# Wide weight splits, fp32r sums over partitions, late norm sums and heads of four in a three-block network

## The chip, the cores and the metric

The kernel runs on one core of a Trainium2 chip. A core has TensorE (matmuls, 128 x 128 stationary operand, results in PSUM), VectorE, ScalarE, GpSimd and SyncE, which run side by side and meet through semaphores; DMA queues bring data from HBM. The metric is the device time of one execution in microseconds (us), the median of several runs.

## The reference

One sequence of 512 positions, width 1024, goes through three blocks and everything is fp32. Cut to its skeleton:

```python
def first_block(x, mem, ...):           # one layer
    proj = _rmsnorm(x, g_in) @ w_in
    o_a = _nsa_mixer(...) * silu(gate_a)        # compressed, block-selected and windowed attention
    o_b = _ssd_mixer(...)                       # chunked state-space scan, conv of 4, RMS norm
    o_c = _memory_attention(...) * silu(gate_x) # cross attention to mem
    return _rmsnorm(x + concat([o_a, o_b, o_c]) @ w_out, g_final)

def second_block(x, ...):               # conv of 31 and gated recurrence (hgrn), mixed
    x = layer_norm(ALPHA * x + mix @ w_out, ...)
    return layer_norm(ALPHA * x + (gelu(conv3(u)) * gv) @ w_ffn_out, ...)

def third_block(x, ...):                # two layers
    for layer in range(2):
        x = x + 0.5 * rms_norm(swiglu(rms_norm(x, g[0]), ...), g[1])
        h = rms_norm(x, g[2])
        h = mlstm_mixer(h, ...) if layer == 0 else diff_attention(h, k_sh, v_sh, ...)
        x = x + rms_norm(h, g[3])
        x = x + 0.5 * rms_norm(swiglu(rms_norm(x, g[4]), ...), g[5])
        gate = sigmoid(rms_norm(x, g[6]) @ w_ple_gate[layer])
        x = x + rms_norm((p[layer] @ w_ple_proj[layer]) * gate, g[7])
        if layer == 0: k_sh, v_sh = shared_kv(x, ...)
    return x
```

## The kernel before

The state x lies transposed: eight tiles of 128 features by 512 positions. Every large product is made from split operands. An fp32 array a is kept as a `Pair` of float32r (fp32r) arrays, hi (a copy that rounds, on ScalarE) and lo = a - hi (on VectorE); `mm3` (lines 125 to 127) makes a product of three fp32r matmuls, hi x hi, hi x lo and lo x hi, that add up in one PSUM bank. `weight` (line 107, its copies on lines 112 and 113) loads up to 1024 columns of weights into one of three raw buffers and splits them in pieces of 512 columns into a ring of 12 hi and 12 lo tiles.

`linear` (line 160) makes output tiles m of 128 features: for each m it runs over the contraction tiles k, then calls the evacuation that takes the PSUM bank away. There are six banks for this and two more (`bank2`) for small things. Two kinds of groups are special. A *head* of 3 or 4 output tiles is run interleaved, k outside and m inside, first on positions 0 to 255 and then on 256 to 511, so that it can use x tiles in halves as they come. A *tail* of 2 or 3 tiles is run with the first half of the positions of all its tiles ahead of the second, so that the norm over the outputs can finish for the first half while the second is multiplied.

Norms divide by a root of a sum over features. `Norm.square` (line 345) squares a tile on ScalarE, `Sums.add` (line 315) adds the squares of the tiles on GpSimd, and a matmul with a matrix of ones in plain fp32 sums over the partitions and spreads the sum to all of them: `Sums.total` (line 328) for what has been added up, line 320 for the last tile where `late` is set. The profile shows such an fp32 matmul as two instructions. `rsqrt` (lines 269 to 273) makes the reciprocal root on ScalarE and corrects it with three VectorE instructions. `Layer` does the same for layer norms.

After each sublayer `post` (lines 461 and 462) updates x for the first half of the positions and all eight tiles, then for the second, and calls `then` for each piece. Mostly that is `Pre.feed`: it splits the piece, scaled by the next norm's gain (lines 142 and 143), and hands it to `Norm.square` for the next norm. The next product uses the split x without the norm's factor; the factor (`pre.row`) is multiplied in at the evacuation. Where the norm is *lazy*, `linear` finishes it half by half, each behind its half of the head's matmuls. `Pre.feed` runs behind eight such posts, once at full width in the first block and once at full width for the second layer of block three.

The queues are not written out by hand. Tile buffers are rings, and a scheduler at build time gives each engine its order of instructions: of those whose inputs and buffers are there by its own cost model, the one that comes first in the program. At run time each engine keeps that order, and an instruction that waits holds back those behind it on its engine.

## Time and profile before

| | us |
|---|---|
| median of three runs | 3583.32 (3582.47 to 3584.28) |
| the profiled execution | 3585.29 |
| its span, first to last instruction | 3583.5 |
| TensorE busy | 3483.7 (97%) |
| VectorE busy | 2055.7 (57%) |
| ScalarE busy | 1539.3 (43%) |
| GpSimd busy | 485.6 (14%) |
| mean granted TensorE clock | 0.989 of full speed |

An engine counts as busy while it has an instruction in work. TensorE's instructions overlap, so that its busy share says that it had work, not how fast it went. "PEld" is the loading of stationary operands, which runs beside the matmuls. Idle time is put down to the instruction whose result was waited for.

### The profile page before, as it was taken

How to read it: one execution, taken by the hardware profiler on the slowest of the kernel's cores; microseconds unless marked ns; L12 is line 12 of the kernel's file. 1: busy time of each engine (PE TensorE's matmuls, PEld its weight loads, DVE VectorE, ACT ScalarE, POOL GpSimd, SP SyncE). 2: the span in 40 equal slices, each digit the busy share in tenths (PEclk: the TensorE clock that was granted, in tenths of full speed). 3: DMA queues.
4: the chain of work that ended last, by engine and by line, in shares of the span. 5: the costliest groups of instructions: out<-in, count | busy, mean ns of one | idle time of the engine just before them, and what ended most of it. 6: DMA issues, size and time to landing. Idle time of an engine off the chain costs nothing. (4 is left out here: it accounts for less than half of the span.)

```text
span 3583.5 us, 48642 instructions
## 1 busy us (share of the span) xinstructions
PE 3483.7 (97%) x18454; PEld 2924.8 (82%) x18454; DVE 2055.7 (57%) x3879; ACT 1539.3 (43%) x2879; POOL 485.6 (14%) x509
## 2 busy tenths in 40 slices
PE   8999899999999999999999999998999999999997
PEld 7677798888788888888887888887888887888886
DVE  6677669895456354633384763439443448673337
ACT  5465544663434243433345443336433335443335
POOL 2000011230110001201110220114010111020112
PEclk9999999999999999999999999999999999999999
DMA  4411242112323333332321133222533323123331
GB/s 146 127 32 58 62 134 77 53 48 74 109 78 101 99 99 96 108 98 95 96 87 60 60 104 102 91 87 83 188 95 100 93 84 94 56 89 96 98 95 65
DMA packets 109714, 323.97 MB, mean 90 GB/s; under 512 B 12328, under 2 KB 28456, under 8 KB 109480
## 3 DMA queue, kind: packets, MB, share of 16 engines
q1 hardware_dynamic: 93648, 299.27, 26.5%
q10 hardware_dynamic: 15832, 21.60, 1.8%
q8 instruction: 145, 2.38, 0.3%
q14 instruction: 89, 0.73, 0.1%
HBM read 308.23 MB, written 12.58 MB: 90 GB/s over the span
## 5 line engine op out<-in xcount | busy, mean ns | idle before, releaser
L125 PE MATMUL ps<-x,hi 128*128 128x512 f32 (+1 forms) x3552 | 1292.3, 366 | 6.6 <-ACT x L142 5.2
L126 PE MATMUL ps<-x,hi 128*128 128x512 f32 (+1 forms) x3552 | 1279.7, 361 | 9.3 <-DVE x L143 8.6
L127 PE MATMUL ps<-x,lo 128*128 128x512 f32 (+1 forms) x3552 | 1275.0, 360 | 1.6 <-DVE lo L113 1.6
L112 ACT CAST hi<-raw 128x512 fp32r<-128x512 f32 (+1 forms) x1112 | 668.8, 612 | 1265.9 <-PE ps L126 1119.8
L113 DVE TENSOR_TENSOR lo<-raw,hi 128x512 fp32r<-128x512 f32 (+1 forms) x1112 | 784.8, 715 | 714.3 <-ACT hi L112 712.1
L126 PEld LDWEIGHTS ps<-x,hi 128*128 128x128 f32 x3552 | 674.8, 190 | 113.2 <-DVE x L143 16.3
L125 PEld LDWEIGHTS ps<-x,hi 128*128 128x128 f32 x3552 | 671.5, 190 | 107.6 <-ACT x L142 9.2
L127 PEld LDWEIGHTS ps<-x,lo 128*128 128x128 f32 x3552 | 673.6, 190 | 101.8 <-issue 2.5
L125 PE MATMUL ps<-h,hi 128*128 128x512 f32 (+1 forms) x990 | 367.1, 371 | 0.0
L127 PE MATMUL ps<-h,lo 128*128 128x512 f32 (+1 forms) x990 | 364.0, 368 | 0.0
L126 PE MATMUL ps<-h,hi 128*128 128x512 f32 (+1 forms) x990 | 361.2, 365 | 0.0
L485 POOL TENSOR_TENSOR gt<-gt,gt 128x512 f32<-128x512 f32 x88 | 137.7, 1566 | 1090.3 <-DVE gt L484 954.8
L127 PEld LDWEIGHTS ps<-h,lo 128*128 128x128 f32 x990 | 185.8, 188 | 34.3
L126 PEld LDWEIGHTS ps<-h,hi 128*128 128x128 f32 x990 | 185.9, 188 | 33.2
L125 PEld LDWEIGHTS ps<-h,hi 128*128 128x128 f32 x990 | 186.2, 188 | 30.6
L315 POOL TENSOR_TENSOR sqa<-sqa,sq 128x256 f32<-128x256 f32 (+1 forms) x171 | 166.1, 971 | 293.8 <-ACT sq L345 285.6
L140 DVE TENSOR_TENSOR h<-gt,h 128x512 fp32r<-128x512 f32 x110 | 76.7, 700 | 148.9 <-ACT h L139 146.9
L139 ACT CAST h<-gt 128x512 fp32r<-128x512 f32 x110 | 68.1, 620 | 182.6 <-POOL gt L485 174.4
L484 DVE TENSOR_TENSOR gt<-ps,rbc 128x512 f32<-128x512 f32 x88 | 60.7, 690 | 119.4 <-PE ps L127 119.4
L143 DVE SCALAR_TENSOR_TENSOR x<-x,c,x 128x256 fp32r<-128x256 f32 (+1 forms) x144 | 96.5, 676 | 22.4 <-ACT x L142 22.4
L479 DVE TENSOR_TENSOR gt<-ps,rbc 128x512 f32<-128x512 f32 x88 | 60.8, 690 | 79.9 <-PE ps L127 78.6
L142 ACT ACTIVATE x<-x,c 128x256 fp32r<-128x256 f32 (+1 forms) x144 | 75.4, 528 | 72.4 <-DVE x L462 57.3
(630 smaller groups left out, 3975.4 us busy)
## 6 DMA issues: line engine op xcount, KB each, us to landing
raw<-fi SPq DMA_DIRECT2D x220, 512.0 KB, 3.5
raw<-fo SPq DMA_DIRECT2D x80, 512.0 KB, 3.5
raw<-fo SPq DMA_DIRECT2D x80, 192.0 KB, 2.3
raw<-out SPq DMA_DIRECT2D x16, 512.0 KB, 3.6
raw<-qf SPq DMA_DIRECT2D x16, 512.0 KB, 3.6
raw<-mz SPq DMA_DIRECT2D x16, 512.0 KB, 3.5
raw<-pg SPq DMA_DIRECT2D x16, 512.0 KB, 3.5
raw<-mr SPq DMA_DIRECT2D x9, 512.0 KB, 3.6
```

What stands on the lines that cost most here:

```text
L112: nc.scalar.copy(hi[:, :b], raw[:, a:a + b])
L113: nc.vector.tensor_tensor(lo[:, :b], raw[:, a:a + b], hi[:, :b].bitcast(F32), ALU.subtract)
L125: mm(out, lhs.hi, rhs.hi, start=start, stop=False)
L126: mm(out, lhs.hi, rhs.lo, start=False, stop=False)
L127: mm(out, lhs.lo, rhs.hi, start=False, stop=stop)
L139: nc.scalar.copy(hi, x)
L140: nc.vector.tensor_tensor(lo, x, hi.bitcast(F32), ALU.subtract)
L142: nc.scalar.mul(hi, x, g)
L143: nc.vector.scalar_tensor_tensor(lo, x, g, hi.bitcast(F32), ALU.mult, ALU.subtract)
L315: nc.gpsimd.tensor_tensor(self.acc[:, sl], self.part[h][:, sl], s[:, sl], ALU.add)
L479: nc.vector.tensor_tensor(t, q, pre.row, ALU.mult)
L485: nc.gpsimd.tensor_tensor(u, u, hold[0], ALU.mult)
```

## The change

- `weight` splits a load of up to 1024 columns with one copy and one subtraction into one of 6 hi and 6 lo tiles of 1024 columns. `linear` cuts a contraction of 11 or 12 tiles into loads of 6 (before: of 8).
- The sum over partitions, `ones_sum`, splits its operand into an fp32r pair and takes two fp32r matmuls with an fp32r matrix of ones. The split tiles share the ring of the squares, which grows from 2 to 3 buffers. The layer norm's sum of centred squares stays as it is.
- The adds of `Sums.add` go to VectorE where they are half a tile wide or where the norm is marked `fast`; at full width the others stay on GpSimd.
- `Pre.feed` only splits. `Pre.finish` squares all eight x tiles at full width, adds them on VectorE and finishes the norm; `linear` calls it behind both halves of the head, ahead of the evacuations.
- The mLSTM's first product and the gate product have heads of 4 instead of 3; the gate's tail has 2 tiles instead of 3.

```diff
-        self.wsp = e(tc.tile_pool(name="wsp", bufs=12))
+        self.wsp = e(tc.tile_pool(name="wsp", bufs=6))
...
+        self.onesr = self.const.tile([P, P], F32R, name="onesr")
+        nc.scalar.copy(self.onesr, self.ones)
...
-        bufs = 4 if tag == "gt" else bufs
+        bufs = {"gt": 4, "sq": 3}.get(tag, bufs)
...
-        ps = []
-        for a in range(0, n, 512):
-            b = min(512, n - a)
-            hi = self.wsp.tile([P, 512], F32R, tag="hi", name=self.name("hi"))
-            lo = self.wsp.tile([P, 512], F32R, tag="lo", name=self.name("lo"))
-            nc.scalar.copy(hi[:, :b], raw[:, a:a + b])
-            nc.vector.tensor_tensor(lo[:, :b], raw[:, a:a + b], hi[:, :b].bitcast(F32), ALU.subtract)
-            ps.append(Pair(hi, lo))
-        return ps
+        hi = self.wsp.tile([P, 1024], F32R, tag="hi", name=self.name("hi"))
+        lo = self.wsp.tile([P, 1024], F32R, tag="lo", name=self.name("lo"))
+        nc.scalar.copy(hi[:, :n], raw[:, :n])
+        nc.vector.tensor_tensor(lo[:, :n], raw[:, :n], hi[:, :n].bitcast(F32), ALU.subtract)
+        return Pair(hi, lo)
...
+    def ones_sum(self, q, s, sl, start, stop):
+        nc = self.nc
+        p = Pair(*(self.tmp.tile([P, 512], F32R, tag="sq", name=self.name("os"), bufs=3)[:, sl] for _ in range(2)))
+        nc.scalar.copy(p.hi, s[:, sl])
+        nc.vector.tensor_tensor(p.lo, s[:, sl], p.hi.bitcast(F32), ALU.subtract)
+        nc.tensor.matmul(q[:, sl], self.onesr, p.hi, start=start, stop=False)
+        nc.tensor.matmul(q[:, sl], self.onesr, p.lo, start=False, stop=stop)
...
+        step = kt if kt <= 8 else 6
...
-                    if pre and pre.norm.lazy:
-                        pre.norm.finish(sl)
+                if pre:
+                    pre.finish()
                 for m in ms:
                     evac(m, qs[m], FULL)
...
-            self.acc = self.acc or c.t512("sqa", bufs=3)
-            nc.gpsimd.tensor_tensor(self.acc[:, sl], self.part[h][:, sl], s[:, sl], ALU.add)
+            self.acc = self.acc or c.t512("sqa", bufs=2)
+            eng = nc.gpsimd if sl == FULL and not self.fast else nc.vector
+            eng.tensor_tensor(self.acc[:, sl], self.part[h][:, sl], s[:, sl], ALU.add)
...
-            nc.tensor.matmul(self.q[h][:, sl], c.ones, s[:, sl], start=False, stop=True)
+            c.ones_sum(self.q[h], s, sl, False, True)
...
-        self.c.nc.tensor.matmul(q[:, sl], self.c.ones, self.part[hs[0]][:, sl], start=True, stop=stop)
+        self.c.ones_sum(q, self.part[hs[0]], sl, True, stop)
...
-        self.norm = Norm(c, len(x), late=False, lazy=lazy)
+        self.norm = Norm(c, len(x), late=False, lazy=True, fast=True)
 
     def feed(self, k, sl=FULL):
         self.xg[k] = self.c.split(self.x[k], self.g[:, k:k + 1], tag=f"x{k}", into=self.xg[k], sl=sl)
-        self.norm.square(self.x[k], sl)
+
+    def finish(self):
+        if self.norm.row is None:
+            for t in self.x:
+                self.norm.square(t)
+            self.norm.finish()
...
-        c.linear(w_rows, KD, pre.xg, ev, head=3, pre=pre)
+        c.linear(w_rows, KD, pre.xg, ev, head=4, pre=pre)
...
-        c.linear(w_gate, KD, pre.xg, ev, head=3, tail=3, pre=pre)
+        c.linear(w_gate, KD, pre.xg, ev, head=4, tail=2, pre=pre)
```

## Rows read from the trace of the kernel before

**Rows 1.** The page's first part: busy time (share of the span) and instructions.

```profile
PE 3483.7 (97%) x18454; PEld 2924.8 (82%) x18454; DVE 2055.7 (57%) x3879; ACT 1539.3 (43%) x2879; POOL 485.6 (14%) x509
```

**Rows 2.** Busy time of each engine (x instructions) in stretches around the heads.

```profile
core 0: us, PE busy (x) PEld busy (x) DVE busy (x) ACT busy (x) POOL busy (x), PEclk, DMA share, GB/s
1053.00:1077.00 24.00, 24.00 (x198) 23.87 (x197) 18.69 (x51) 9.98 (x26) 0.00 (x0) 1.00 0.14 44
1436.00:1465.00 29.00, 28.02 (x214) 26.84 (x212) 20.43 (x43) 18.48 (x46) 9.09 (x10) 1.00 0.20 66
1806.00:1831.00 25.00, 21.35 (x154) 19.21 (x153) 25.00 (x50) 13.96 (x36) 12.49 (x26) 1.00 0.00 1
2052.00:2076.00 24.00, 23.56 (x183) 22.17 (x182) 24.00 (x46) 12.60 (x33) 10.85 (x14) 1.00 0.00 1
2417.00:2444.00 27.00, 22.86 (x160) 20.11 (x159) 27.00 (x53) 14.44 (x37) 10.73 (x14) 1.00 0.13 40
2476.00:2510.00 34.00, 29.80 (x201) 27.89 (x202) 33.34 (x58) 22.00 (x50) 18.05 (x19) 0.90 0.12 40
2952.00:2982.00 30.00, 24.43 (x161) 21.48 (x160) 28.48 (x58) 15.65 (x38) 13.73 (x18) 0.95 0.14 41
```

**Rows 3.** Timeline of TensorE, 512 columns: start, duration, instruction.

```profile
400.21 0.39 PE L127 MATMUL ps<-x,lo 128*128 128x512 f32 x1
400.44 0.39 PE L125 MATMUL ps<-x,hi 128*128 128x512 f32 x1
```

**Rows 4.** Timelines of VectorE and GpSimd in a post and at the kernel's end.

```profile
1808.50 0.47 DVE L143 SCALAR_TENSOR_TENSOR x<-x,c,x 128x256 fp32r<-128x256 f32 x1
...
1810.50 1.00 DVE L143 SCALAR_TENSOR_TENSOR x<-x,c,x 128x256 fp32r<-128x256 f32 x1
...
1810.49 3.36 POOL L315 TENSOR_TENSOR sqa<-sqa,sq 128x256 f32<-128x256 f32 x4 [0.53 <-ACT sq L345]
...
3578.59 0.74 DVE L461 TENSOR_TENSOR gt<-e,rbc 128x256 f32<-128x256 f32 x2
3579.26 0.86 DVE L462 SCALAR_TENSOR_TENSOR x<-gt,c,x 128x256 f32<-128x256 f32 x2
```

**Rows 5.** TensorE's waits: us in total, times, longest.

```profile
PE pt L328 <- POOL sqa L315: 26.8, 25, 6.7
```

**Rows 6.** Groups at full width: xcount, busy us, mean ns, idle before.

```profile
L345 ACT ACTIVATE sq<-x 128x512 f32<-128x512 f32 x22 | 13.6, 626 | 6.0 <-POOL sqa L315 5.5 <-DVE x L953 0.4
...
L113 DVE TENSOR_TENSOR lo<-raw,hi 128x512 fp32r<-128x512 f32 x1032 | 740.5, 728 | 665.1 <-ACT hi L112 662.9 <-PE ps L127 0.7 <-PE pt L240 0.5
...
L270 ACT ACTIVATE rbc<-pt,cc 128x512 f32<-128x512 f32 x8 | 5.5, 687 | 3.7 <-PE pt L320 3.5 <-PE pt L328 0.2
```

**Rows 7.** Timeline of TensorE at a full-width and a half-width fp32 sum.

```profile
45.89 1.02 PE L328 MATMUL pt<-sqa,ones 128*128 128x512 f32 x2
46.34 0.68 PE L125 MATMUL ps<-x,hi 128*128 128x256 f32 x1
46.86 0.28 PE L126 MATMUL ps<-x,hi 128*128 128x256 f32 x1
...
2466.79 0.60 PE L320 MATMUL pt<-sq,ones 128*128 128x256 f32 x2
2467.04 0.47 PE L126 MATMUL ps<-x,hi 128*128 128x256 f32 x1
2467.34 0.28 PE L127 MATMUL ps<-x,lo 128*128 128x256 f32 x1
```

**Rows 8.** Groups of half-width fp32 sums by shape; two instructions make a sum.

```profile
L328 PE MATMUL pt<-sqa,ones 128*128 128x256 f32 x78 | 26.7, 425 | 20.1 <-POOL sqa L315 20.1
...
L320 PE MATMUL pt<-sq,ones 128*128 128x256 f32 x36 | 12.7, 437 | 0.0
...
L320 PE MATMUL pt<-x,ones 128*128 128x256 f32 x8 | 2.6, 412 | 0.0
```

**Rows 9.** Busy time and granted clock (PEclk) in a stretch, as rows 2.

```profile
2501.00:2505.00 4.00, 3.79 (x20) 3.79 (x21) 4.00 (x8) 2.02 (x5) 2.21 (x2) 0.58 0.40 135
```

More of the change, by code (lines that the diff above doesn't have):

```diff
@@ L160, in mm @@
             def mm(m, k, sl):
-                if (m, k // 8) not in ws:
-                    a = k // 8 * 8
-                    ws[m, k // 8] = self.weight(w[m][:, a * P:min(a + 8, kt) * P])
-                o = (k % 4) * P
-                self.mm3(qs[m][:, sl], ws[m, k // 8][k % 8 // 4][:, o:o + P], x[k][:, sl], k == 0, k == ks[-1])
+                c = k // step
+                if (m, c) not in ws:
+                    ws[m, c] = self.weight(w[m][:, c * step * P:min(c * step + step, kt) * P])
+                o = (k - c * step) * P
+                self.mm3(qs[m][:, sl], ws[m, c][:, o:o + P], x[k][:, sl], k == 0, k == ks[-1])
             first = head and ms[0] == 0
@@ L197, in linear_t @@
                     wt = self.weight(w[cb, k // 2])
-                rhs = wt[k % 2]
+                rhs = wt[:, k % 2 * 512:k % 2 * 512 + 512]
                 for t in range(nt):
@@ L294, with __init__ @@
 class Sums:
-    def __init__(self, c, n, late):
-        self.c, self.n, self.late = c, n, late and n > 1
+    def __init__(self, c, n, late, fast=False):
+        self.c, self.n, self.late, self.fast = c, n, late and n > 1, fast
         self.left = [n, n]
@@ L334, with __init__ @@
 class Norm:
-    def __init__(self, c, n, eps=EPS, late=True, lazy=False):
+    def __init__(self, c, n, eps=EPS, late=True, lazy=False, fast=False):
         self.c, self.n, self.eps, self.lazy = c, n, eps, lazy
-        self.sums = Sums(c, n, late and not lazy)
+        self.sums = Sums(c, n, late and not lazy, fast)
         self.row = None
@@ L411, in parts @@
         for k in range(kt):
-            c.mm3(q, t[4][k // 4][:, k % 4 * P:(k % 4 + 1) * P], x[k], k == 0, k == kt - 1)
+            c.mm3(q, t[4][:, k * P:(k + 1) * P], x[k], k == 0, k == kt - 1)
             if k == kt - 1:
@@ L431, with __init__ @@
 class Pre:
-    def __init__(self, c, x, g, lazy=False):
+    def __init__(self, c, x, g):
         self.c, self.x, self.g = c, x, g
         self.xg = [None] * len(x)
-        self.norm = Norm(c, len(x), late=False, lazy=lazy)
+        self.norm = Norm(c, len(x), late=False, lazy=True, fast=True)
     def feed(self, k, sl=FULL):
         self.xg[k] = self.c.split(self.x[k], self.g[:, k:k + 1], tag=f"x{k}", into=self.xg[k], sl=sl)
-        self.norm.square(self.x[k], sl)
+    def finish(self):
[3 more added lines that the diff above has]
+            self.norm.finish()
     @property
     def row(self):
-        if self.norm.row is None:
-            self.norm.finish()
+        self.finish()
         return self.norm.row
@@ L818, in go @@
                 for k in range(2):
-                    c.mm3(q, ws[k][m // 4][:, m % 4 * P:m % 4 * P + P], ps[k], k == 0, k == 1)
+                    c.mm3(q, ws[k][:, m * P:m * P + P], ps[k], k == 0, k == 1)
                 t = c.t512("gt")
@@ L1925, in third @@
     for i in range(2):
-        nxt = Pre(c, x, g(i, 2), lazy=i == 0)
+        nxt = Pre(c, x, g(i, 2))
         ffn3(c, x, pre, g2(i, 1), a[f"fi_3{i}0"], a[f"fo_3{i}0"], nxt.feed)
-        pre, nxt = nxt, Pre(c, x, g(i, 4), lazy=True)
+        pre, nxt = nxt, Pre(c, x, g(i, 4))
         if i == 0:
@@ L1938, in third @@
             pre, nxt = nxt, Pre(c, x, g(1, 0))
-            kv = Pre(c, x, vec[:, 136:144], lazy=True)
+            kv = Pre(c, x, vec[:, 136:144])
             e = ple[i].load(pp)
@@ L1967, in body @@
         g2 = lambda i, j: half[:, 64 * i + 8 * j:64 * i + 8 * j + 8]
-        pre = Pre(c, x, g(0, 0), lazy=True)
+        pre = Pre(c, x, g(0, 0))
         ple = [Ple(c, a[f"pT{i}"], a[f"pp{i}"], [dram.tile([P, 512], F32, name=c.name("ed")) for _ in range(KD)])
```

## The prediction

> **What bounds the kernel now.** I read the page's busy times first: TensorE is busy 97% of 3583.5 us, VectorE 57% [rows 1]. A busy TensorE is not yet a full one, because matmul records overlap, so the second view is a count: in the undisturbed stretch of 256-column fp32r matmuls from 1053 to 1077, 198 instructions take 24.00 us [rows 2], 0.121 us each; at 512 columns one starts every 0.23 us [rows 3]. With these two pitches any stretch can be priced: instructions times pitch is work, the rest is waiting. Nearly everywhere the weights' product fills the time, so neither loads, splits nor evacuations are on the path there. What is left to win is (a) matmuls that cost more than they must and (b) the places where TensorE starves.
>
> (b) sits behind the residual updates. There `post` computes x in halves, `Pre.feed` splits each half-tile and squares it for the next norm, and the next product's head eats the split tiles. The stretch at 1053 is such a head whose feeder has no norm sums: GpSimd busy 0, TensorE full. Its siblings with norm sums hold, in instructions x 0.12: 154 in 25 us (6.5 us lost), 160 in 27 (7.8; the head at 3509 repeats this, same count), 161 in 30 (10.7), 201 in 34 (9.9), 214 in 29 (3.3), 183 in 24 (2.0; the head at 3144 repeats this) [rows 2]. Together 6.5 + 2 x 7.8 + 10.7 + 9.9 + 3.3 + 2 x 2.0 = 50 us in eight heads. Some 512-column matmuls are counted at 0.12 there, so this is a little high. VectorE is busy all of the 25 or 27 us, GpSimd 9 to 18 us. Why VectorE is slow there: the same half-width split takes 0.47 us at 1808.50 and 1.00 us at 1810.50, while GpSimd adds squares from 1810.49 to 1813.85; with GpSimd idle, at the kernel's end, two multiplies start every 0.67 us and two updates take 0.86 [rows 4]. TensorE also waits 26.8 us in 25 places for GpSimd's sums themselves, 6.7 of it in one place [rows 5].
>
> **The change, part by part.**
>
> *Norm sums after the head, on VectorE.* `Pre.feed` keeps only the split. Per tile half VectorE then needs 0.34 + 0.40 + 0.40 = 1.13 us [rows 4], the split taken like the update; 16 of them are 18 us, where it now takes 25 us or more. A head of four is 192 matmuls x 0.12 = 23 us, so TensorE, not VectorE, should set the pace, as at 1053. Still, about two wide weight splits and the half-width norm correction fall into the same time, some 3 to 4 us. Bounds for what remains per head: 0.2 us (the undisturbed head) to 6.2 us (50/8, as now). I take 2.7, nearer to the undisturbed one since the GpSimd work that separates the two is gone: 8 x 2.7 = 22 left of 50, **-28 us** (bounds -48 and 0).
>
> What that moves: eight squares, seven adds, one split of the sum, two matmuls and the reciprocal root now stand behind the head, and no evacuation can start before. In TensorE's queue the ones matmuls stand before whatever the scheduler did not put ahead of them. Chain from the last split to the first free bank, with full-width durations [rows 6]: square 0.63, add 0.73, split 0.63 + 0.73, ones 0.45, root 0.69, three corrections 2.2, evacuation 0.7: 6.8 us; with six more adds behind the post (4.4) 11.2; with two wide weight subtractions between (2 x 1.46) 14.1. Cover: the head's last 12 matmuls (1.45 us) and two more tiles in the two free banks (2 x 24 x 0.227 = 10.9): 12.3 us. So 0 to 2 us a head shows; it is in the 2.7.
>
> *Ones sums in fp32r.* A full-width fp32 sum at 45.89 pushes the stream back by 46.86 - 45.89 - 0.12 = 0.85 us, a half-width one at 2466.79 by 0.55 - 0.12 = 0.43 [rows 7]. Of half-width sums there are (78 + 36 + 8)/2 = 61 [rows 8], of full-width ones 14 by the code (eight in the mLSTM heads, two each in `ssd` and `Conv`, two of `Pre`): 61 x 0.43 + 14 x 0.85 = 38 us. After it, 16 half sums of the eight heads are 8 full ones, and a sum is two fp32r matmuls: 45 x 0.24 + 22 x 0.45 = 21 us. **-17 us**; up to -24 where a sum starts after a wait, and -10 if a part of these sums lies in waits anyway. The price is a copy on ScalarE and a subtraction on VectorE ahead of each sum, 0.8 us at half width and 1.4 at full. Inside a tail the other half's matmuls hide it; behind an 8-tile contraction the other half is 48 x 0.12 = 5.8 us, less than the chain from evacuation to the first split tile, so there it shows: six such posts x 0.65 us = +4.
>
> *Half-width adds on VectorE in the tails.* A half-width add of 0.84 us on GpSimd (four in 3.36) becomes one of about 0.35, like the multiply of the same width [rows 4]. The waits for sums outside the eight head stretches and without the 6.7 us at the SSD norm (full width, stays on GpSimd) are some 13 us. The split of the sum takes its place there, so half goes: **-6 us** (0 to -13).
>
> *Wide splits, six slots.* ScalarE and VectorE are far from full, so the saved instructions are worth nothing on the path; the kernel's first weight arrives half as fine, +0.5. The same bytes in six slots are coarser: the first block's output product has a head of four with 12 contraction tiles, now eight wide tiles in six slots. The last two cannot be split until the first finish both halves; 2 to 3 us of other matmuls stand between, and the split needs 2.5: +2.5 (0 to 6). The feed-forward outputs hold three weights instead of four; a weight lasts 33 x 0.23 = 7.5 us and its splits some 3, so nothing.
>
> *Heads of four, tails of two.* The mLSTM's head gains 5.8 us of cover (in the 2.7 above). The last tail's half shrinks from 8.6 to 5.8 us, so the final post starts later against the last matmul: +1.
>
> Sum: -28 - 17 - 6 + 4 + 0.5 + 2.5 + 1 = **-43 us**. The profiled execution took 3585.3 us (span 3583.5), 2.0 above the median of 3583.3; 3585.3 - 43 = 3542, against the median **3540**.
>
> **A rule weighed.** The row shows VectorE's split at 1.00 us while GpSimd adds, 0.47 otherwise [rows 4]. The Trainium skill, GPSIMD Engine Reference, Performance versus the Vector engine, has a two-input add about 1.96 times slower on GpSimd than on VectorE and explains it by GpSimd's own software; it names no cost to VectorE. By that rule alone the adds would come to an engine that is already the slow one in these stretches. What it would give is the first rival; the row speaks against it.
>
> **The rivals.** *VectorE stays the feeder.* Its 25 us hold seven more adds (7 x 0.6 = 4.2) and the weight splits, and the scheduler puts them between the post's own: 18 + 4 + 4 = 26 us, and only some 1 us a head is won. Then -17 - 8 - 3 + 8 = -20: 3563. For it: VectorE is at 100% in these stretches. Against: the undisturbed head. Chance 0.15.
> *The row comes late.* TensorE's order is fixed before the run; if the ones matmuls wait for squares that queue behind weight splits, or three square buffers chain the adds to ScalarE, TensorE stands at the end of each of nine heads. The break-even is 43/9 = 4.8 us of standing per head above what is in the sum, that is, a chain of about 19 us instead of 11 to 14. At 8 us it gives 3540 + 72 = 3612. The trace shows that a standing TensorE also loses clock: it is granted 0.58 in the four microseconds behind the starved head at 2481 to 2501 [rows 9], and such stretches would be seen more often. For it: 26.8 us of such waits now. Against: a chain of 14 with every queue counted. Chance 0.11.
> *Slots starve the output products.* With fewer, larger slots each of 80 feed-forward output tiles could wait 0.5 us: +40, 3580, no change. Chance 0.06.
>
> **How the numbers follow.** Forecast case 0.68 at 3540, its own range 3518 to 3562. The 8-in-10 range is 3515 to 3572: it takes in the first rival, and leaves out the late row and the far end of the gains. A difference under 0.2% (7 us) can't be told from none here. Faster: 0.68 + 0.15 = 0.83; the same 0.06; slower 0.11.
>
> **What would show it.** In the profile after: GpSimd busy near 0 in head stretches, VectorE's split at 0.4 to 0.5 us throughout, 192 matmuls in 23.5 to 26 us; no wait of TensorE for GpSimd's sums but at the SSD norm; each ones sum at two fp32r pitches. Wrong would be: heads as long as now (first rival), or a new wait of the ones matmuls for the split sum, or of the seventh tile for a bank, above 2 us a head (second), or waits of w_out's matmuls for weight splits (third).

## The result, and the profile after

The kernel after takes 3564.5 us (median; 3563.8 to 3564.6) against 3583.2: a ratio of 0.9947, with a 95% interval of 0.993 to 0.9964. That is 18.7 us gained where 43 were forecast. The sign was right and the time lies inside the range, but more than half of the gain is missing. Ratios below have intervals of about 0.0015 to either side, so kernels that were not timed together compare to some 5 us.

First the page of the kernel after, the line that answers to [rows 1]:

```profile
PE 3469.0 (97%) x18462; PEld 2921.0 (82%) x18462; DVE 2036.4 (57%) x3509; ACT 1481.6 (42%) x2354; POOL 401.7 (11%) x352
```

Then four of the head stretches, as [rows 2] (busy time of each engine and its instructions; PEclk is the granted clock), and below them two stretches behind a stop, as [rows 9]:

```profile
core 0: us, PE busy (x) PEld busy (x) DVE busy (x) ACT busy (x) POOL busy (x), PEclk, DMA share, GB/s
1792.00:1817.00 25.00, 24.54 (x190) 23.24 (x190) 24.79 (x58) 13.94 (x29) 1.77 (x12) 1.00 0.19 54
2034.00:2058.00 24.00, 24.00 (x189) 23.95 (x189) 23.28 (x55) 12.80 (x26) 0.00 (x0) 0.93 0.07 23
2400.00:2425.00 25.00, 24.51 (x189) 23.21 (x189) 23.03 (x55) 11.16 (x24) 0.00 (x0) 1.00 0.27 89
2931.00:2953.00 22.00, 20.22 (x150) 18.54 (x150) 21.84 (x57) 12.97 (x27) 2.09 (x4) 1.00 0.10 28
...
2453.00:2456.00 3.00, 3.00 (x14) 3.00 (x15) 1.64 (x3) 1.00 (x3) 0.00 (x0) 0.50 0.82 205
...
2460.00:2467.00 7.00, 4.55 (x18) 3.97 (x19) 6.75 (x19) 5.49 (x12) 0.00 (x0) 0.50 0.09 32
```

GpSimd has all but left the heads (2.1 us at most, where it had 9 to 18). Three of these four hold 189 or 190 matmuls in 24 or 25 us, where the same heads before had 154 in 25, 183 in 24 and 160 in 27 [rows 2]; the fourth holds 150 in 22, before 161 in 30. Last TensorE's waits (us in total, times, longest), as [rows 5]:

```profile
PE pt L133 <- ACT os L131: 21.7, 14, 4.3
PE ps L123 <- ACT hi L111: 10.2, 1, 10.2
PE ps L1710 <- DVE st L1700: 4.9, 2, 3.9
PE ps L1382 <- DVE q L1376: 4.4, 1, 4.4
PE ps L123 <- ACT s L146: 4.4, 1, 4.4
PE ps L750 <- issue: 4.3, 1, 4.3
...
PE pt L134 <- DVE os L132: 2.3, 6, 0.9
```

The waits for GpSimd's sums are gone by name, and 21.7 + 2.3 us of waits for the copy and the subtraction of the same sums stand in their place. New are 4.4 us ahead of the first block's scores (L1382, its queries come late) and 4.3 ahead of the differential attention's first scores (L750). The 4.4 us for a split at L146 stand where the kernel before waited 6.7 us for GpSimd's sum, at the SSD norm.

**Where the time went.** I split each trace into work and waits. Work is every TensorE instruction at the pitch of its shape (fp32r 0.227 us at 512 columns, 0.120 at 256; fp32 0.43 and 0.22 per instruction; narrow ones by their columns). Waits are what the starts of consecutive instructions lie further apart than that. The waits are sorted by place: *posts*, from the first update of x of one of the eight posts that go half by half to 6 us behind its last; *tails*, the 20 us ahead of such a post; *early*, all ahead of the first tail, some 1780 us; *behind*, the rest. Seven of the eight heads with norm sums lie in the posts; the eighth post, at the end, has no product behind it, and the eighth head, at 1436 before and 1412 after, lies in the early stretch. Some 24 us ahead of the first matmul and behind the last stand in no column.

Each line is one traced execution, and the time beside it is the median of all. The trace of a_narrow is its slowest execution, 3562.0 us against a median of 3554.3. The traces of n_first and mix have the same instructions on TensorE and VectorE up to 2.9 ms, and their early waits differ by 4.7 us: a difference of that size in one column can't be told from none.

| us | time | work | early | tails | posts | behind |
|---|---|---|---|---|---|---|
| before | 3583.2 | 3437.8 | 57.7 | 12.5 | 44.1 | 6.9 |
| after | 3564.5 | 3420.4 | 48.1 | 29.6 | 21.8 | 19.7 |
| b_late | 3567.4 | 3437.7 | 58.6 | 23.1 | 6.1 | 21.4 |
| b_ones | 3603.3 | 3420.3 | 51.9 | 25.4 | 64.1 | 13.5 |
| b_wide | 3608.8 | 3437.8 | 52.2 | 17.6 | 61.4 | 10.0 |
| a_vec | 3552.7 | 3420.4 | 43.0 | 23.5 | 18.3 | 21.6 |
| a_narrow | 3554.3 | 3420.4 | 52.4 | 31.9 | 10.7 | 21.1 |
| a_early | 3579.0 | 3420.4 | 49.6 | 36.6 | 36.2 | 15.6 |
| a_tail32 | 3568.9 | 3433.8 | 42.0 | 24.9 | 24.0 | 20.8 |
| a_norow | 3546.7 | 3420.4 | 41.4 | 22.2 | 18.4 | 18.0 |
| v_narrow | 3544.2 | 3420.4 | 45.6 | 25.1 | 8.4 | 21.4 |
| v_fp32 | 3549.5 | 3438.0 | 41.6 | 10.2 | 24.1 | 13.5 |
| n_fp32 | 3534.4 | 3438.0 | 39.7 | 11.6 | 4.8 | 15.4 |
| n_first | 3528.1 | 3438.0 | 29.2 | 11.4 | 6.0 | 15.7 |
| mix | 3521.6 | 3438.0 | 33.9 | 11.3 | 8.1 | 9.5 |
| b_vec | 3530.0 | 3437.8 | 34.2 | 11.3 | 15.7 | 7.5 |
| b_dummy2 | 3577.5 | 3437.8 | 42.3 | 11.3 | 52.0 | 8.4 |

The first two lines say where the gain went. Work fell by 17.4 and the posts by 22.3: together 39.7, nearly the forecast. But the tails took back 17.1 and the stretches behind the heads 12.8; early 9.6 were won, 3.2 of them at the head at 1436 (3.6 us of waits before, 0.4 after, by the same split). -17.4 - 22.3 + 17.1 + 12.8 - 9.6 = -19.4, against 20.8 between the two spans.

One of the taking-back places is the gate product. The timeline of the kernel after there (start, duration, engine, line; in brackets idle time before and what ended it):

```profile
2419.20 5.52 ACTq L843 DMA_DIRECT2D e<-ed  x5
...
2420.82 0.47 DVE L150 SCALAR_TENSOR_TENSOR x<-x,c,x 128x256 fp32r<-128x256 f32 x1
...
2424.82 2.82 ACT L354 ACTIVATE sq<-x 128x512 f32<-128x512 f32 x5 [5.11 <-DMA raw<-pg]
...
2434.87 0.69 DVE L281 SCALAR_TENSOR_TENSOR rbc<-rbw,rbc 128x512 f32<-128x512 f32 x1
...
2436.62 2.48 DVE L852 TENSOR_TENSOR gt<-ps,rbc 128x512 f32<-128x512 f32 x4
...
2443.30 1.28 POOL L324 TENSOR_TENSOR sqa<-sq,sq 128x512 f32<-128x512 f32 x1 [57.28 <-ACT sq L354]
2444.66 6.10 POOL L324 TENSOR_TENSOR sqa<-sqa,sq 128x512 f32<-128x512 f32 x4
...
2448.51 0.28 PE L125 MATMUL ps<-x,lo 128*128 128x256 f32 x1
...
2452.10 0.41 DVE L324 TENSOR_TENSOR sqa<-sqa,sq 128x256 f32<-128x256 f32 x1
...
2452.54 0.40 ACT L131 CAST os<-sqa 128x256 fp32r<-128x256 f32 x1 [1.48 <-DVE sqa L324]
...
2453.00 0.58 PE L133 MATMUL pt<-os,onesr 128*128 128x256 f32 x1 [4.21 <-ACT os L131]
```

From the end of the last split of the head (2421.3) to the finished row (2435.6) it takes 14.3 us; the squares stand behind 5.5 us of DMA issues on ScalarE. Only then are four tiles set free at once, and their sigmoids, products, squares and GpSimd's adds (1.3 to 1.5 us each) run until 2450.8, two microseconds after the first half of the tail has been multiplied. The half add, the copy and the ones matmul follow, and TensorE has stood for 4.2 us. Eight microseconds on it stands again for 4.3.

### The profile page after: what moved, and what is told of

Read it like the earlier page. It is cut to its first block, busy times and chain, and to the rows that moved or that the text cites. A ratio compares the mean times of both kernels' runs of the same rounds, so it can differ in the third digit from the quotient of the medians.

```text
span 3562.7 us, 47180 instructions
## 1 busy us (share of the span) xinstructions
PE 3469.0 (97%) x18462; PEld 2921.0 (82%) x18462; DVE 2036.4 (57%) x3509; ACT 1481.6 (42%) x2354; POOL 401.7 (11%) x352
## 4 chain that ended last, share of the span: by engine, by line
PE 83%; DVE 11%; ACT 3%; issue 1%; DMA 1%; POOL 1%; ACTq 0%; POOLq 0%; DVEq 0%; SPq 0%
PE ps L123 24%; PE ps L125 24%; PE ps L124 24%; DVE lo L112 2%; DVE ca L1597 2%; PE ps L750 1%; PE pt L248 1%; DVE x L476 1%; DVE e L1659 1%; PE ps L1676 1%; DVE gt L475 1%; PE ps L767 1%; PE ps L1098 1%; DVE x L150 1%; POOL sqa L324 1%
## 5 line engine op out<-in xcount | busy, mean ns | idle before, releaser
L111 ACT CAST hi<-raw 128x1024 fp32r<-128x1024 f32 (+3 forms) x604 | 582.9, 968 | 1278.5 <-PE ps L124 1103.9
L112 DVE TENSOR_TENSOR lo<-raw,hi 128x1024 fp32r<-128x1024 f32 (+3 forms) x604 | 708.2, 1176 | 541.7 <-ACT hi L111 538.2
L499 POOL TENSOR_TENSOR gt<-gt,gt 128x512 f32<-128x512 f32 x88 | 169.9, 1932 | 1222.1 <-ACT hi L111 591.2
L146 ACT CAST h<-gt 128x512 fp32r<-128x512 f32 x110 | 68.3, 621 | 180.8 <-POOL gt L499 178.1
L1597 DVE SCALAR_TENSOR_TENSOR ca<-cp,c,ca 128x512 f32<-128x512 f32 x120 | 89.1, 784 | 0.2
L240 ACT ACTIVATE e<-ps,e 128x128 f32<-128x128 f32 (+3 forms) x128 | 66.8, 529 | 37.2 <-DVE e L238 15.7
```

Of the source, the lines that this page charges most:

```text
L111: nc.scalar.copy(hi[:, :n], raw[:, :n])
L112: nc.vector.tensor_tensor(lo[:, :n], raw[:, :n], hi[:, :n].bitcast(F32), ALU.subtract)
L146: nc.scalar.copy(hi, x)
L240: nc.scalar.activation(e[:, 0:n], q[:, 0:n], AF.Exp, bias=mx[:, 0:1], scale=scale, accum_out=mx[:, 1:2])
L499: nc.gpsimd.tensor_tensor(u, u, hold[0], ALU.mult)
L1597: eng.scalar_tensor_tensor(a, p[:, k:k + 512], cw[:, i, k:k + 1], a, ALU.mult, ALU.add)
```

## The experiments

Names: *late* are norm sums behind the head, *wide* the weight splits of 1024 columns, *split sums* the fp32r ones sums. Kernels named b_ are the kernel before with something of the change, a_ the kernel after without something, v_ build on a_vec and n_ on n_fp32. My theory at first (A): each part is worth what the sum gave it, and what is missing went where a late row meets a short product.

**One part of the change alone, on the kernel before.**

b_ones (split sums alone; the rings of squares and of running sums as in the kernel after):

```diff
-            nc.tensor.matmul(self.q[h][:, sl], c.ones, s[:, sl], start=False, stop=True)
+            c.ones_sum(self.q[h], s, sl, False, True)
...
-        self.c.nc.tensor.matmul(q[:, sl], self.c.ones, self.part[hs[0]][:, sl], start=True, stop=stop)
+        self.c.ones_sum(q, self.part[hs[0]], sl, True, stop)
```

> The kernel before with the fp32r ones sums alone (split of the sum, two fp32r matmuls, a third square buffer, one buffer of running sums less); adds stay on GpSimd, half by half in the heads. Theory A (each part is worth what the sum gave it, and the missing 25 us went where a norm's row comes late for work that is not a long product): TensorE's work falls by 17 us, the longer chain to the sum gives back some 4: 3570 us, range 3566 to 3575. Rival B (the copy and the subtraction ahead of each sum give back in waits what the matmuls save): 3580 to 3586, with 10 us or more of new waits for the copy of the sum.

Measured: 3603.3, ratio 1.0055 (1.0042 to 1.0067). It is slower by 20 us, beyond either expectation: work is 17.5 us less, as priced, but the posts wait 20 more and the tails 13. The waits for the copy of a sum are 29.2 us. Theory A fails here, and rival B is too mild.

b_late (the late sums alone, their adds on VectorE, with heads and tails as before):

```diff
     def feed(self, k, sl=FULL):
...
-        self.norm.square(self.x[k], sl)
+
+    def finish(self):
+        if self.norm.row is None:
+            for t in self.x:
+                self.norm.square(t)
+            self.norm.finish()
```

> The kernel before with the late norm sums alone: the feed only splits, the eight squares, the adds on VectorE and the fp32 ones sums come behind both halves of the head; heads stay at 3, tails as they were, weight splits narrow. Theory A: the heads gain some 24 us as in the kernel after, the first block's queries, the differential attention's queries and the gate give back some 10: 3569, range 3564 to 3574. Rival E (the late row costs nothing by itself; the gate's head of 4 with a tail of 2 makes the new waits): 3559, range 3555 to 3563.

Measured: 3567.4, ratio 0.9955 (0.9941 to 0.9968), as theory A has it and outside rival E. The heads are nearly clean: 6.1 us in all posts, where 44.1 were. But 25 us come back, 10.6 in the tails and 14.5 behind the heads, with gates at their old 3 and 3. The late row itself brings them.

b_wide (wide splits alone):

```diff
-        self.wsp = e(tc.tile_pool(name="wsp", bufs=12))
+        self.wsp = e(tc.tile_pool(name="wsp", bufs=6))
...
+        nc.scalar.copy(hi[:, :n], raw[:, :n])
+        nc.vector.tensor_tensor(lo[:, :n], raw[:, :n], hi[:, :n].bitcast(F32), ALU.subtract)
```

> The kernel before with the wide weight splits alone (6 slots of 1024 columns, contractions of 11 and 12 tiles in loads of 6). Theory A: no change, 3583 within 3. Rival D (coarse slots hold up ScalarE's queue, and wide subtractions run beside GpSimd's adds and stretch both): slower, 3590 or more, with the loss in the heads and in the tails of the output products.

Measured: 3608.8, ratio 1.0072 (1.0059 to 1.0084): rival D. 17.3 of the 25 us lie in the posts, where TensorE's waits for split tiles rise from 8.6 to 14.9 us. Two of the three parts tried lose 20 and 25 by themselves, the third wins 16, and all of it together wins 19: the parts act on one another, so that prices taken singly don't add up.

**GpSimd's remaining adds.** a_vec is the kernel after with all norm adds on VectorE:

```diff
-            eng = nc.gpsimd if sl == FULL and not self.fast else nc.vector
+            eng = nc.vector
```

> The kernel after with every add of the norm sums on VectorE, full width too. Rival C (what is given back in the tails is GpSimd's full-width adds, 1.3 to 2.2 us each beside VectorE's wide subtractions): the waits at the mLSTM's output, at both gates and at the SSD norm fall by 6 to 12 us: 3552 to 3559. Theory A (the late row and the length of the chain): 3561 to 3566, no change.

Measured: 3552.7, ratio 0.9917 (0.9903 to 0.993), 12 us less than the kernel after: rival C. Tails fall by 6, early by 5, posts by 3.5.

**One part taken out of the kernel after.** a_narrow has the weight splits as before (the diff of b_wide, reversed).

> The kernel after with the weight splits put back to pieces of 512 columns (12 slots, loads of 8), all else as after. By itself the wide split cost the kernel before 25 us. Theory F (formed on the first four runs: the wide split and the split of the sum lose only where GpSimd adds beside VectorE, in heads and tails; with the heads freed of GpSimd only the tails still pay): 3556, range 3551 to 3561, with the gain in the waits at the mLSTM's output and the gates. Rival G (the wide split costs its 25 us wherever it stands): 3540 or less. Theory A (no effect): 3562 to 3567.

Measured: 3554.3 (its runs lie between 3549 and 3562), ratio 0.992 (0.9908 to 0.9933), 10 us less, at the size that theory F has. Its one trace, at 3562.0, is only 2.5 us shorter than that of the kernel after, so it can't place all of the gain. In it the posts fall from 21.8 to 10.7, and the tails, where theory F has the gain, don't fall. With GpSimd gone from the heads a wide subtraction still stands for 1.2 us ahead of a half-tile's split in VectorE's queue, here in the kernel after:

```profile
1809.14 1.22 DVE L112 TENSOR_TENSOR lo<-raw,hi 128x1024 fp32r<-128x1024 f32 x1
1810.28 0.47 DVE L150 SCALAR_TENSOR_TENSOR x<-x,c,x 128x256 fp32r<-128x256 f32 x1
```

v_narrow below decides this.

a_g33 undoes the gate's head and tail:

```diff
-        c.linear(w_gate, KD, pre.xg, ev, head=4, tail=2, pre=pre)
+        c.linear(w_gate, KD, pre.xg, ev, head=3, tail=3, pre=pre)
```

> The kernel after with the gate product at a head of 3 and a tail of 3 as before. TensorE waits some 14 us around each of the two gates in the kernel after, 6 in the kernel before. Theory H (the tail of 2 gives the first half's sum only 5.8 us of cover): both gates win 3 to 5 us: 3556, range 3552 to 3560. Theory A (the late row sets free all evacuations at once, whatever the tail): 3562 to 3567.

Measured: 3565.0, ratio 0.995 (0.9938 to 0.9963), no change: theory H falls. The length of the tail is not what holds the gates.

a_early puts the squares back into the feed:

```diff
         self.xg[k] = self.c.split(self.x[k], self.g[:, k:k + 1], tag=f"x{k}", into=self.xg[k], sl=sl)
+        self.norm.square(self.x[k], sl)
...
-            for t in self.x:
-                self.norm.square(t)
```

> The kernel after with the squares of a head's norm taken again in the feed, half by half, and added on VectorE there; the sum and the row still come behind the head. The row then comes some 8 us earlier at the first block, the gates and the differential attention (some 15 us of waits in all there), but VectorE has 0.42 us more per half-tile: 16 x 1.55 = 25 us for a head's post against 23 us of matmuls. Theory F: the heads lose 2 to 4 us each, the late places win back 8: 3574, range 3566 to 3582. Rival I (the late row is the dearer of the two): 3552 to 3560.

Measured: 3579.0, ratio 0.9989 (0.9981 to 0.9998), as theory F has it. The posts lose 14 again, but the late places don't win back the 8 that it has: behind the heads 4 are won, and the tails lose 7 more. It isn't a full test of the late row, since the ones sums still come behind the head, and the wait of 4.4 us for the first queries stands.

a_tail32 has plain fp32 sums in tails:

```diff
-            c.ones_sum(self.q[h], s, sl, False, True)
+            nc.tensor.matmul(self.q[h][:, sl], c.ones, s[:, sl], start=False, stop=True)
```

(and likewise in `total` where the last tile is still to come.)

> The kernel after with plain fp32 sums where the norm is summed in a tail (the two matmuls of a half-width sum at 0.43 us in place of a copy, a subtraction and two fp32r matmuls at 0.24); sums behind heads stay split. TensorE waits 21.7 us for the copies of sums in the kernel after. Rival B (the copy and the subtraction are what is given back): the matmuls cost 30 x 0.2 = 6 us more, the waits fall by 12 to 16: 3557, range 3553 to 3561. Theory F (the waits are for GpSimd's adds ahead of the copy and stay): 3567 to 3572.

Measured: 3568.9, ratio 0.9956 (0.9943 to 0.997), theory F. Work rises by 13.4, more than the 6 that I had counted, and waits fall by 7.5. The waits for the copy become waits for the running sum: 15.7 us for VectorE's adds and 6.1 for GpSimd's.

a_norow tells what the late row costs. The norm's factor is left out of three products:

```diff
-            nc.vector.tensor_tensor(t[:, sl], q[:, sl], pre.row[:, sl], ALU.mult)
+            nc.vector.tensor_tensor(t[:, sl], q[:, sl], pre.x[0][:, sl], ALU.mult)
```

(and the same at the evacuations of the first block's and the differential attention's queries.)

> The kernel after in which the evacuations of the first block's queries, of the differential attention's queries and of the gates multiply by the first tile of x in place of the norm's row: the norm's factor is left out of these three products, the row is still made, nothing else changes. Theory J (what is given back is the late row where the next product is short): the wait of 4.4 us at the first queries, some 6 at the differential attention and 10 to 14 at the two gates go: 3542, range 3537 to 3549. Theory C (GpSimd's adds in the tails are the whole of it): 3556 to 3563.

Measured: 3546.7, ratio 0.9903 (0.9888 to 0.9917), 17.8 us less than the kernel after: theory J. The two waits for queries have left the head of the list of waits. By the split of the traces some 6 us are won at the first queries, 5 behind the head of the differential attention and 6 in the tails of the two gates, where 10 to 14 had been expected.

**Two parts taken out.** v_narrow is a_vec with narrow splits.

> Every norm add on VectorE (3552.7 with wide splits) and the weight splits narrow again. Theory F (wide splits lose only beside GpSimd's adds): with none of these adds left the width is worth nothing, 3552 within 4. Rival G (the wide split costs its own 10 us in the kernel after, by coarse slots and by a VectorE instruction of 1.2 us ahead of a waiting split or sum): 3543 within 4, with the heads' loss falling from 18 us to 7.

Measured: 3544.2, ratio 0.9896 (0.9879 to 0.9912), 8.5 less than a_vec: rival G, and theory F falls in this point. The posts go from 18.3 to 8.4. So the wide split costs this without GpSimd's norm adds, too. That it is the grain of the instructions, and not the coarser slots, isn't shown by a run of its own; for the grain speaks that TensorE's waits for split weights come to 1.9 us in all in the kernel after, but for the one at the start.

v_fp32 is a_vec with plain fp32 sums everywhere.

> Every norm add on VectorE, wide splits, and all ones sums in plain fp32 again. By the prediction's term the fp32r sums are worth 17 us of TensorE's work, all of it: 3570. Theory F (in the tails and behind the heads the copy and the subtraction give back some 7 of the 17): 3563, range 3559 to 3567. Rival B (they give back all): 3553 or less.

Measured: 3549.5, ratio 0.9909 (0.9894 to 0.9923). This is 3 us below a_vec, not to be told from none: rival B. TensorE's longest waits for sums (a_vec first, then v_fp32):

```profile
PE pt L133 <- ACT os L131: 15.4, 11, 3.7
```

```profile
PE pt L329 <- ACT sq L354: 5.1, 2, 3.9
PE pt L337 <- DVE sqa L324: 4.7, 7, 1.9
```

Work is 17.6 us more and waits 17 less: 13.3 less in the tails and 8.1 behind the heads, and 5.8 more in the posts. The fp32r sums save exactly the matmul time that I gave them, and the copy and the subtraction ahead of them spend it.

v_rows is a_vec with the loads of e, keys and values issued by GpSimd, and the first block's norm finished ahead of its head:

```diff
-            self.c.nc.scalar.dma_start(e[m], self.dram[m])
+            self.c.nc.gpsimd.dma_start(e[m], self.dram[m])
...
         pre.feed(k)
+    pre.finish()
     nsa.tables()
```

> Every norm add on VectorE; besides, the loads of e at the gates and of keys and values in the differential attention are issued from GpSimd's queue in place of ScalarE's, where they stand for 5.5 us ahead of the squares, and the first block's norm is finished ahead of the head of its queries. Theory J (the row's chain sets these places): the wait of 4.4 us for the first queries goes, the gates' waits fall by 3 to 5 us each, 3541, range 3536 to 3547. Rival K (the evacuations that the row sets free, not its own time, fill the gates): 3548, only the 4.4 us. If GpSimd's issuing disturbs VectorE: 3555 or more.

Measured: 3553.0, ratio 0.992 (0.9905 to 0.9935), no gain over a_vec and between what theory J and rival K have and what was expected of a disturbed VectorE. Early falls by 4.4 and the tails by 7.2, and behind the heads 10.2 come back, half of it at the differential attention. Three edits in one kernel were too many to read more than this out of it.

**All three taken out.** n_fp32 is the kernel after with all adds on VectorE, narrow splits and fp32 sums.

> Late norm sums and every norm add on VectorE, heads of four, with narrow weight splits and plain fp32 sums: of the change only the late sums, the heads and the engine of the adds are left. If the costs are separate: 3552.7 - 8.5 (narrow) - 3.2 (fp32) = 3541, and by the excess of TensorE in the two traces, posts 8 in place of 24, 3536; range 3534 to 3543. If narrow and fp32 heal the same waits: 3544 to 3549.

Measured: 3534.4, ratio 0.9867 (0.985 to 0.9883), as expected of separate costs. Taken singly they are 11.8 + 8.5 + 3.2 = 23.5 us, together 30, so they at least don't heal the same waits. n_first has `pre.finish()` ahead of the first block's head besides.

> As the kernel with late sums, VectorE adds, narrow splits and fp32 sums, and the first block's norm finished ahead of the head of its queries. Theory J (a late row in front of a short product shows in full): 4 us less than without, some 3536. If the ones sum ahead of the head stalls the head for the same time: no difference.

Measured: 3528.1, ratio 0.9848 (0.9833 to 0.9863), 6 less. n_h33 is n_fp32 with heads of 3 and the gate's tail of 3 as before.

> As the kernel with late sums, VectorE adds, narrow splits and fp32 sums, with the heads of the mLSTM's rows and of the gates at 3 and the gates' tail at 3 as in the kernel before. By the prediction's terms (5.8 us of cover at the mLSTM, 2.9 less at the last tail) within 3 us of it; if the gate's tail of two costs its 2.9 us of cover in full at both gates, 6 us less.

Measured: 3537.8, ratio 0.9875 (0.986 to 0.989): 3 us, not to be told from none.

**The engine of the adds alone.** b_vec is the kernel before with one line changed:

```diff
-            nc.gpsimd.tensor_tensor(self.acc[:, sl], self.part[h][:, sl], s[:, sl], ALU.add)
+            nc.vector.tensor_tensor(self.acc[:, sl], self.part[h][:, sl], s[:, sl], ALU.add)
```

> The kernel before with every norm add on VectorE and nothing else changed: squares and adds stay in the feed, half by half. Theory F (GpSimd's adds beside VectorE are the price, wherever they stand): VectorE then needs 16 x 1.55 = 25 us a head, as long as now, while the tails and waits for GpSimd's sums (26.8 us) win: 3570, range 3564 to 3577. If the late sums are what counts: 3580 or more. If the engine of the adds alone is what counts: 3560 or less.

Measured: 3530.0, ratio 0.9854 (0.9839 to 0.9869). This one word gains 52 us, nearly three times the whole change, with squares and adds in the feed as ever. The posts lose 15.7 in place of 44.1 and no row is late.

b_vec and n_h33, timed together, differ by the late sums alone (and by a buffer of squares and one of running sums): all norm adds on VectorE, heads and tails of three, narrow splits and fp32 sums in both. The one with late sums takes 3537.8, the other 3530.0, and their runs don't overlap (3533.9 to 3539.5, 3528.3 to 3530.9). So once the adds are on VectorE, late sums at every head lose 8 us: by the split of the traces the posts win 8, and 10 are lost behind the heads and 6 early.

Whether the sums just come sooner or VectorE itself runs freely is told by b_dummy2: b_vec, and in the feed an add on GpSimd that nobody waits for. (One buffer of running sums less makes room for its result.)

```diff
+        t = self.c.t512("scr", bufs=1)
+        self.c.nc.gpsimd.tensor_tensor(t[:, sl], self.x[k][:, sl], self.x[k][:, sl], ALU.add)
         self.norm.square(self.x[k], sl)
```

> The kernel before with every norm add on VectorE (3530), and in the feed of the heads one more add per half-tile on GpSimd, of x to itself into a scratch tile that nobody reads (and one buffer of running sums less, to make room). Theory F (GpSimd's adds slow VectorE's updates and splits in the same stretch): the heads lose again what they lost before, 16 in excess become some 44: 3558, range 3548 to 3570, with splits at 0.9 to 1.0 us. Rival L (the sums came late because GpSimd's adds are slow themselves): 3530 within 4.

Measured: 3577.5, ratio 0.9987 (0.9978 to 0.9996). 47 us are gone again, 36 of them in the posts; that is theory F's side, but some 8 us beyond its range. The groups by shape (line, engine, operation, count; busy us, mean ns), before, b_vec and b_dummy2 in this order: the half-width split of x, the half-width add, and the last two corrections of the reciprocal root, of which the first reads PSUM (pt).

```profile
L315 POOL TENSOR_TENSOR sqa<-sqa,sq 128x256 f32<-128x256 f32 x124 | 99.5, 803 | 157.0 <-ACT sq L345 149.7 <-PE ps L127 3.4 <-DVE x L143 0.4
L143 DVE SCALAR_TENSOR_TENSOR x<-x,c,x 128x256 fp32r<-128x256 f32 x128 | 84.2, 662 | 0.2 <-ACT x L142 0.2
...
L272 DVE SCALAR_TENSOR_TENSOR rbw<-pt,rbw 128x256 f32<-128x256 f32 x39 | 16.3, 417 | 0.6
L273 DVE SCALAR_TENSOR_TENSOR rbc<-rbw,rbc 128x256 f32<-128x256 f32 x39 | 20.6, 528 | 0.4
```

```profile
L143 DVE SCALAR_TENSOR_TENSOR x<-x,c,x 128x256 fp32r<-128x256 f32 x128 | 60.5, 477 | 0.8 <-ACT x L142 0.3
...
L315 DVE TENSOR_TENSOR sqa<-sqa,sq 128x256 f32<-128x256 f32 x124 | 51.7, 417 | 5.2 <-ACT sq L345 5.2
...
L272 DVE SCALAR_TENSOR_TENSOR rbw<-pt,rbw 128x256 f32<-128x256 f32 x39 | 16.3, 419 | 0.5
L273 DVE SCALAR_TENSOR_TENSOR rbc<-rbw,rbc 128x256 f32<-128x256 f32 x39 | 16.3, 418 | 0.3
```

```profile
L442 POOL TENSOR_TENSOR scr<-x 128x256 f32<-128x256 f32 x128 | 106.5, 832 | 684.3 <-DVE x L464 566.6 <-DVE x L1466 115.0
...
L143 DVE SCALAR_TENSOR_TENSOR x<-x,c,x 128x256 fp32r<-128x256 f32 x128 | 81.8, 643 | 0.3 <-ACT x L142 0.3
```

The split takes 0.48 us on average without GpSimd's adds and 0.64 to 0.66 with them (0.9 to 1.0 had been expected), whether these are of use or not. An engine that nobody waits for takes VectorE's time. How much: the 452 splits, products, updates and adds of the eight posts take 202.6 us in b_vec and 241.4 in b_dummy2, 39 us more, against 36 us more that TensorE waits there. So the stretched instructions, and not the buffer, account for the loss in the posts.

The trace of the kernel before, sorted by what GpSimd does, shows the form of it. A split takes 473 ns when no GpSimd arithmetic runs beside it (39 of 128), 500 when such an instruction starts after it has begun (41), and 954 when one is already under way (48).

And one head stretch of each, b_vec first:

```profile
2386.00:2412.00 26.00, 25.11 (x177) 22.84 (x176) 25.62 (x68) 14.61 (x38) 0.00 (x0) 1.00 0.16 51
```

```profile
2406.00:2434.00 28.00, 24.95 (x160) 20.50 (x159) 28.00 (x63) 13.89 (x36) 11.86 (x14) 1.00 0.08 21
```

With 68 VectorE instructions in 26 us b_vec gives TensorE 177; with GpSimd's 14 beside them VectorE does 63 in 28.

**A version with both kinds of sums.** mix is n_first with the norm ahead of the differential attention squared and summed in the feed again:

```diff
+        if self.early:
+            self.norm.square(self.x[k], sl)
...
-        nxt = Pre(c, x, g(i, 2))
+        nxt = Pre(c, x, g(i, 2), early=i == 1)
```

> As the kernel with late sums, VectorE adds, narrow splits, fp32 sums and the first block's norm finished ahead of its head (3528), with the norm ahead of the differential attention squared and summed in the feed again, half by half on VectorE. Theory J: of the 11.6 us of TensorE's excess behind that head some 8 go, its head loses 2 to 3 more: 3522, range 3518 to 3526. If the late row is not what holds up the differential attention's first scores: 3528 to 3532.

Measured: 3521.6, ratio 0.9831 (0.9818 to 0.9844), the lowest median of all, and at the size expected: behind the heads 9.5 in place of 15.7, against 2.1 more in the posts. The step from n_first is 6.5 us between medians and some 4 in the two traces, behind the early stretch, so it lies at the edge of what can be told; so do the 8 us below b_vec, which has shorter heads besides. With n_h33 against b_vec this speaks for late sums ahead of long products and against them ahead of short ones; it wasn't tried head by head.

## Why the prediction was right and wrong

Set against the sum, the gains came and the costs were too small. The heads gave 22.3 in the posts and 3.2 at the head at 1436, the work 17.4, and the rest of the early stretch 6.4: 49 us, where -28, -17 and -6 make 51. For all costs together the sum had +8 (4 + 0.5 + 2.5 + 1), and the tails and the stretches behind the heads took 29.9. The steps that failed are the prices of what stands in those two places: the copy and the subtraction ahead of a sum, and the cover of the row's chain.

- **The heads (-28).** Right: 22 us were to be left in eight heads, and they hold 20 (19.6 of the 21.8 in the posts, and 0.4 at the one in the early stretch). GpSimd is out of them, the split takes 475 ns on average, the matmuls flow. The reason given, GpSimd's adds beside VectorE [rows 4], is the one that b_dummy2 shows.
- **A term that was missing: the adds left on GpSimd.** The prediction saw the contention, priced it in the heads alone, and took the late sums for its cure. Full-width adds stay on GpSimd in the change, and the sum had no term for them; a_vec puts them at 12. They stood there before the change too, so this is partly a gain not taken, and not only a cost that came. And b_vec shows that the engine of the adds alone takes the heads most of the way, with VectorE as the feeder: the first rival's picture, VectorE busy through the whole head, but at only some 2 us lost per head, since its instructions are short again.
- **Ones sums (-17): a step that failed.** The work is right, 17.4. The price of the copy and the subtraction was mis-sized: +4 for six posts, while v_fp32 shows 17 us of waits against the same sums in fp32, 13.3 of them in the tails. "Inside a tail the other half's matmuls hide it" was the wrong step. At the gate above, the first half's matmuls are done at 2448.8 and its last add is not until 2452.5; the copy comes behind that, and TensorE stands through it.
- **The row's chain (0 to 2 us a head, within the 2.7): the other step that failed.** The chain was sized nearly rightly: up to 14.1 us with the evacuation, so 13.4 to the finished row, and the gate's takes 14.3 to there. The cover was not: 12.3 us of further tiles exist only where the product is long. The first block's queries and the differential attention's are read at once by scores, and a gate has four tiles left, whose evacuations pile up in front of its own norm's sum. a_norow puts this at 18 us, in the three places that it frees. I forecast one cover for all heads, from the long ones.
- **Wide splits (+3, start and slots).** Mis-sized: 8.5 to 10 in the kernel after, and mostly in the posts. Costing them at nothing in the heads ("far from full") looked at the average: VectorE isn't full over the kernel, but in a head a subtraction of 1.2 us stands ahead of a split of 0.47 that TensorE needs. That this grain is the whole of it is argued, as said at v_narrow.
- **Half-width adds (-6), heads of four and tail of two.** The adds were not tried by themselves; the 6.4 us that the early stretch won beside its head are of their size, but may be in part the spread of one trace. Heads and tail weigh nothing that can be measured (a_g33, n_h33).
- **The rivals.** The row that comes late (3612) did come, at three kinds of places and not at nine, and so it ate half of the gain in place of all of it. Starved output products: no, for TensorE's waits on split weights are 10.2 us at the start (9.7 before) and 1.9 in two places besides. The first rival's number, 3563, lies within 2 us of the measured time, but by luck: it had the heads nearly as long as before, and they lose 20 us in place of 48.
- **The rule weighed.** A two-input add takes 803 ns on GpSimd and 417 on VectorE here, a ratio of 1.93, so the 1.96 that the Trainium skill has (GPSIMD Engine Reference, Performance versus the Vector engine) holds. I went by the row against that page's silence on VectorE, and that was right; but another page of the skill speaks. The Trainium skill, SBUF — State Buffer, SBUF: two separate sides, says that VectorE with two SBUF inputs and GpSimd take a shared port pair in turn, each for a whole instruction. The trace of the kernel before agrees: with a GpSimd instruction already under way the split, with two SBUF inputs, takes 954 ns in place of 473, and the last correction of the root (L273, two SBUF inputs) 954 in place of 419, while the correction before it, of the same size with one input in PSUM (L272), takes 411 in place of 421 (8 and 5 cases). No run here tried the port by itself.

What stays open: why split sums alone cost the kernel before 20 us in its heads (their copies and subtractions fall between VectorE's splits there, but that was only argued), how much of the wide splits' cost is their grain, and where the loads moved to GpSimd lose at the differential attention what they win at the gates.

## What to carry to other kernels

When two engines disturb each other, move the operation first, by itself: the shift of one line gained more than a redesign around it. A chain behind a head is covered by what the next product still has to do, so price it for each product, the shortest first; moved behind every head alike, the sums lost 8 us here once the engine was right. And ahead of a sum that is waited for, even a cheap preparation can show as a wait, while matmul time saved there may be time in which TensorE would have stood.

## What the runs showed of the hardware

An engine nobody waits for isn't free: 128 half-width and 16 full-width adds on GpSimd, 127 us of its time, cost the program 47 us. It acts through VectorE: in the kernel before, the split takes 954 ns in place of 473 where a GpSimd instruction is already under way. And a stop can cost more than its length: behind the 4.2 us of standing from 2448.8 in the kernel after, the granted clock is 0.50 from 2453 to 2456, the lower of the two levels (1.2 and 2.4 GHz), and it still is from 2460 to 2467, behind the second stop. 256-column matmuls start every 0.21 us there in place of 0.12, some 3 us more for the thirty-odd of them. [rows 9] had shown the same behind a starved head.
